# A mixture-of-experts stage whose low-row experts get plain transposes instead of a transposing matmul that adds

## The chip, the cores and the metric

One core of a Trainium2 chip runs the whole program. The metric is the device time of one execution in microseconds (us); a kernel's time is the median of its runs. TensorE (PE) does matmuls, with its weight loads shown as PEld; VectorE is DVE, ScalarE is ACT, GpSimd is POOL, SyncE is SP.

## The reference, cut to what matters

Two layer blocks run on 256 tokens of width 1024. The change lies in the last large step, a mixture of 8 experts in which each token goes to two of them:

```
def moe_swiglu(h, w_router, w1, w3, w2):
    t = h.reshape(B * S, D)
    ...
    for e in range(N_EXPERTS_2):
        out = out + gates[:, e:e + 1] * swiglu(t, w1[e], w3[e], w2[e])

def swiglu(h, w1, w3, w2):
    return (jax.nn.silu(h @ w1) * (h @ w3)) @ w2
```

w1 and w3 are 1024 x 3584 and w2 is 3584 x 1024 for each expert, all float32.

## The kernel before, in words

`moe` handles each expert's own tokens alone. `gather` collects them into at most 128 slots, as a high part (fp32r) and a low part (what fp32r lost); slot i*64+s stands at position 2s+i. Whether an expert has more than 64 rows is known only at run time, so matmuls stand twice, in the two arms of a branch that `arms` builds and TensorE's sequencer takes: "many" (over 64 rows) and "few". In the trace L1613 is the up matmul of many, L1610 that of few; L1641 is the transpose of many, L1639 its counterpart of few. By these lines experts 0, 1 and 4 have many rows here, and experts 2, 3, 5, 6 and 7 few.

An expert's 3584 hidden columns are done in two halves of 1792 (NS = 2); half number i is 2e+s for expert e, s = 0 or 1. A half is made of jobs of two weight tiles of 128 x 1792 (896 KB) each:

- 4 jobs of w1 and 4 of w3 ("up"). Each tile is loaded into `raw` (9 buffers), ScalarE rounds it into `whi` (L99), VectorE subtracts to get `wlo` (L100); 4 buffers of each. TensorE multiplies the gathered rows by both. In a few expert the 64 high rows and the 64 low rows lie side by side as one stationary operand of 128, so the product has the high rows' result on partitions 0 to 63 and the low rows' on 64 to 127, and the two have still to be added. `evict` copies w1's banks to `gs` and w3's to `us` (L1828).
- `turn`: `gs` and `us` are transposed in blocks of 128 x 128, 14 of each per half, in four pieces (8, 8, 8 and 4 blocks). For a many expert that is a transpose (L1641). For a few expert it is a matmul of the block with the constant `both` (L1639), whose even columns hold two ones, so that the two halves are added while the block is transposed; the result lies in even columns.
- `turned` follows each piece: ScalarE makes the silu of the gate's bank `pts[0]` into `sg` (L1822), and VectorE multiplies it by the other bank into `hd` (L1823). `hd` has one buffer, so the first write for half i waits until the down matmuls of half i-1 have read the last one.
- 4 jobs of w2 ("down", L1629), straight from `raw`, with `hd` as the stationary operand.

The order on TensorE is: up of half i with the four pieces of half i-1 among its w1 jobs, then down of half i-1, then up of half i+1. At s = 0 the pieces of the half before belong to another expert and have a branch of their own; at s = 1 they stand inside the branch of the up job. After the last half of an expert `finish` adds its result to the tokens (`dh`, `dl`, L1659, L1664). A scheduler decides the order within each engine; each engine then takes its instructions in that fixed order. Weight loads are issued by SP in the order of the jobs, each as soon as its buffer of `raw` is free.

In what follows a **stretch** runs from the first down matmul of one half to the first of the next: it has 8 down tiles and then 16 up tiles. A first-half stretch is one whose up tiles are of s = 0, a second-half stretch one of s = 1.

Of the kernel before, what the change touches and what calls it, by code (L numbers as in the profile page):

```python
# [8 lines left out]
F32 = mybir.dt.float32  # L9
# [3 lines left out]
AF = mybir.ActivationFunctionType  # L13
ALU = mybir.AluOpType
AX = mybir.AxisListType
PSUM = bass.MemoryType.PSUM
ADD, SUB, MUL = ALU.add, ALU.subtract, ALU.mult
MAX, MIN, EQ = ALU.max, ALU.min, ALU.is_equal

P = 128  # L20
# [1109 lines left out]
class Block2:  # L1130
# [378 lines left out]
    def moe(self, cap=P):  # L1509
# [4 lines left out]
        K, nc, tc, a, x = self.K, self.K.nc, self.K.tc, self.a, self.x  # L1514
        E, NS, HALF = 8, 2, P // 2
        MS, R = 1792, 7
        BANKS = ((0, 512), (512, 512), (1024, 512), (1536, 256))
        iota = iota_row(K, self.pool, P)

        both = self.T([P, P])  # L1520
        nc.gpsimd.memset(both[:, 1::2], 0.0)
        nc.vector.tensor_tensor(both[:, 0::2], K.ident[:, :HALF], K.ident[:, HALF:], op=ADD)
        up_of = lambda n, e, s, k: a[n][0, e, k * P:(k + 1) * P, s * MS:(s + 1) * MS]

        def down_of(e, s, j):
# [68 lines left out]
        def arms(e, f):  # L1594

            with tc.If(many[e] > HALF) as c:
                f(False)
            with c.Else():
                f(True)
# [15 lines left out]
        def up(few, e, g, to, k, w):  # L1615

            for b, (o, n) in enumerate(BANKS):
                piece(few, g[:, k], w, slice(o, o + n), to[b][:, :n], k == 0, k == KC - 1, b < 2)

        def down(few, s, hd, acc, j, w):  # L1620


            c0 = c = j % 4 * MS
            while c < c0 + MS:
                c1 = min((c // 512 + 1) * 512, c0 + MS)
                r, h = divmod(c // 512, 2)
                o = slice((r + h) % 2 * HALF, (r + h) % 2 * HALF + HALF) if few else slice(0, P)
                n = 2 if few else 1
                mm(acc[h][o, c % 512:c % 512 + c1 - c], hd[:, j // 4 * R + r, ::n], w[0][:, c - c0:c1 - c0],  # L1629
                   start=s == 0 and j < 4 and r < n and c % 512 == 0,  # L1630
                   stop=s == NS - 1 and j > 3 and r >= R - n and c1 % 512 == 0)
                c = c1

        def turn(few, rows, pt, c0):

            for c in range(c0, min(c0 + 4, 2 * R)):
                z = rows[:, c // R * (MS // 2) + c % R:(c // R + 1) * (MS // 2):R]
                if few:
                    mm(pt[:, (c - c0) * P:(c - c0 + 1) * P], z, both, start=True, stop=True)  # L1639
                else:  # L1640
                    nc.tensor.transpose(pt[:, (c - c0) * P:(c - c0 + 1) * P], z, K.ident)  # L1641

        def transposed(e, h):

# [159 lines left out]
        for t in range(NT):  # L1804
            with K.behind(K.last):
                top2_weights(K, self.tmp, *tops[t][:2], iota, comb[:, t, :])
                nc.gpsimd.tensor_scalar(x[:, t, :], x[:, t, :], ALPHA, None, op0=MUL)
        most, mosti = self.T([P, 1]), self.T([P, 1], I32)
        nc.vector.tensor_reduce(most, cnt, axis=AX.X, op=MAX)
        nc.vector.tensor_copy(mosti, most)  # L1810
# [5 lines left out]
        def turned(i, c, pts):  # L1816

            n = min(4, 2 * R - c) * P
            if c == 0:
                hT[i] = self.W([P, 2 * R, P], "hd", F32, 1)  # L1820
            sg = self.W([P, 512], "sg", bufs=1)
            nc.scalar.activation(sg[:, :n], pts[0][:, :n], AF.Silu)  # L1822
            nc.vector.tensor_tensor(hT[i].rearrange("p c s -> p (c s)")[:, c * P:c * P + n], sg[:, :n], pts[1][:, :n], op=MUL)  # L1823
# [7 lines left out]
        for n, (name, e, s, ks) in enumerate(jobs):  # L1831
# [4 lines left out]
            if name == "down":  # L1836
                if s == 0 and q == 0:
                    accs[e] = [K.ps() for _ in range(2)]
                if i == E * NS - 1 and q == 0:
                    for c in range(0, 2 * R, 4):  # L1840
                        pts = [K.ps() for _ in range(2)]
                        arms(e, lambda few: [turn(few, rows, pt, c) for rows, pt in zip(ups[i], pts)])
                        turned(i, c, pts)
                arms(e, lambda few: [down(few, s, hT[i], accs[e], *t) for t in tiles])
                if s == NS - 1 and q == 4:
                    hotT = transposed(e, gs[e][1])
                if s == NS - 1 and q == 6:
                    if e == E - 1:
                        finish_last(e, accs.pop(e), hotT)
                    else:  # L1850
                        ends = finish(e, accs.pop(e), hotT)
                        next(ends)
                continue
# [6 lines left out]
            before = first and i > 0  # L1860
            if before:
                pts = [K.ps() for _ in range(2)]
                turns = lambda few: [turn(few, rows, pt, 2 * q) for rows, pt in zip(ups[i - 1], pts)]
                if s == 0:

                    arms(e - 1, turns)

            def f(few):
                if before and s:
                    turns(few)  # L1870
                for t in tiles:
                    up(few, e, g, banks, *t)
            arms(e, f)
            if before:
                turned(i - 1, 2 * q, pts)
            if q == 6:
# [81 lines left out]
```

## Time and profile before

| | |
|---|---|
| median of 3 runs | 2000.67 us (1997.23 to 2002.16) |
| the profiled execution | 1999.19 us, of which 1997.6 us are the span from first to last instruction |
| PE busy | 1843.4 us (92%) |
| PEld, DVE, ACT, POOL busy | 1450.1, 1133.8, 929.9, 169.8 us |
| HBM read | 543 MB, 272 GB/s over the span |

The expert stage runs from about 942 us to 1958 us of the span. A busy PE is not one at its peak: a row of busy time also holds matmuls that wait for weight loads. Times in the rows below are us from the span's start.

### The profile page before, as it was taken

What the parts mean: (1) busy time and instruction counts of PE and PEld (TensorE: products, weight loads), DVE (VectorE), ACT (ScalarE), POOL (GpSimd) and SP (SyncE); (2) the same over time, 40 slices, a digit from 0 to 9 for tenths busy, and PEclk for the clock granted to TensorE, in tenths of its full rate; (3) what the DMA queues carried; (4) which work ended last, traced back from release to release, by engine and by line L of the source; (5) the groups of instructions that cost most, each with busy time, mean ns of one, the idle gap of its engine ahead of it and who ended that gap; (6) DMA issues with size and microseconds to landing.
All of it is one profiled execution on the core that took longest, in us unless ns stands there. A gap on an engine that the chain in (4) does not pass through costs nothing. (4 is left out here: it accounts for less than half of the span.)

```text
span 1997.6 us, 27678 instructions
## 1 busy us (share of the span) xinstructions
PE 1843.4 (92%) x11023; PEld 1450.1 (73%) x11023; DVE 1133.8 (57%) x1395; ACT 929.9 (47%) x1222; POOL 169.8 (9%) x251
## 2 busy tenths in 40 slices
PE   7988698877999999987999999999999999999997
PEld 6878464323779998776877677877878678787875
DVE  4765542111986555887756436656557455675635
ACT  6444341101474443555746445545555445565533
POOL 2051210000400000324100000000000000000002
PEclk9989789889999999998999999999999999999999
DMA  7000579999655554415888989899989898999982
GB/s 221 29 1 1 193 292 407 421 421 397 243 179 175 190 190 148 169 43 219 323 299 318 327 273 376 319 362 395 360 326 400 306 361 308 387 376 359 405 318 106
DMA packets 131002, 546.58 MB, mean 274 GB/s; under 512 B 13568, under 2 KB 46475, under 8 KB 118540
## 3 DMA queue, kind: packets, MB, share of 16 engines
q1 hardware_dynamic: 126604, 539.21, 71.6%
q10 hardware_dynamic: 3952, 3.84, 0.6%
q8 instruction: 129, 2.11, 0.4%
q0 software_dynamic: 272, 1.05, 0.2%
q14 instruction: 45, 0.37, 0.1%
HBM read 543.01 MB, written 1.05 MB: 272 GB/s over the span
## 5 line engine op out<-in xcount | busy, mean ns | idle before, releaser
L100 DVE TENSOR_TENSOR wlo<-raw,whi 128x1792 fp32r<-128x1792 f32 (+2 forms) x412 | 681.0, 1694 | 291.5 <-ACT whi L99 290.2
L99 ACT ACTIVATE whi<-raw 128x1792 fp32r<-128x1792 f32 (+3 forms) x436 | 582.1, 1382 | 175.6 <-DMA raw<-in_exp_w_dram 59.2
L1610 PE MATMUL ps<-wlo,xg 128*128 128x256 f32 (+1 forms) x960 | 266.5, 308 | 17.0 <-DVE wlo L100 16.7
L1629 PE MATMUL ps<-raw,hd 128*64 128x512 f32 (+3 forms) x1024 | 275.4, 541 | 0.9 <-DVE hd L1823 0.9
L1610 PE MATMUL ps<-whi,xg 128*128 128x256 f32 (+1 forms) x960 | 266.7, 308 | 0.0
L1613 PE MATMUL ps<-whi,xg 128*128 128x512 f32 (+1 forms) x768 | 225.3, 373 | 0.0
L1629 PEld LDWEIGHTS ps<-raw,hd 128*64 128x64 f32 (+1 forms) x1024 | 129.5, 158 | 127.5 <-issue 111.8
L1610 PEld LDWEIGHTS ps<-wlo,xg 128*128 128x128 f32 x960 | 187.8, 196 | 33.5 <-DVE wlo L100 27.2
L1610 PEld LDWEIGHTS ps<-whi,xg 128*128 128x128 f32 x960 | 188.8, 197 | 9.6 <-issue 2.9
L114 PE MATMUL ps<-xTl,whi 128*128 128x256 f32 x576 | 161.4, 282 | 1.4 <-DVE xTl L100 1.4
L1613 PEld LDWEIGHTS ps<-whi,xg 128*128 128x128 f32 x768 | 141.6, 190 | 27.5 <-issue 1.5
L115 PE MATMUL ps<-xTh,wlo 128*128 128x256 f32 x544 | 153.4, 283 | 3.3 <-DVE wlo L100 3.2
L113 PE MATMUL ps<-xTh,whi 128*128 128x256 f32 x544 | 151.4, 281 | 0.4 <-ACT xTh L99 0.4
L1613 PE MATMUL ps<-wlo,xg 128*128 128x512 f32 (+1 forms) x384 | 141.7, 369 | 0.7 <-DVE wlo L100 0.7
L100 POOL TENSOR_TENSOR wlo<-raw,whi 128x448 fp32r<-128x448 f32 (+3 forms) x24 | 39.4, 1666 | 1105.7 <-ACT whi L99 1105.6
L1823 DVE TENSOR_TENSOR hd<-sg,ps 128x512 f32<-128x512 f32 x64 | 39.5, 617 | 127.2 <-PE ps L1629 88.7
L114 PEld LDWEIGHTS ps<-xTl,whi 128*128 128x128 f32 x576 | 108.7, 189 | 3.5 <-DVE xTl L100 2.7
L1822 ACT ACTIVATE sg<-ps 128x512 f32<-128x512 f32 x64 | 34.5, 539 | 162.0 <-PE ps L1639 91.6
L115 PEld LDWEIGHTS ps<-xTh,wlo 128*128 128x128 f32 x544 | 104.0, 191 | 5.7 <-DVE wlo L100 5.6
L113 PEld LDWEIGHTS ps<-xTh,whi 128*128 128x128 f32 x544 | 102.3, 189 | 1.7 <-ACT xTh L99 0.9
L1105 PE MATMUL ps<-dn,hT 128*32 128x512 f32 x256 | 70.3, 664 | 19.2 <-DMA dn<-in_w_down_dram 19.2
L1613 PEld LDWEIGHTS ps<-wlo,xg 128*128 128x128 f32 x384 | 73.0, 190 | 15.0 <-DVE wlo L100 1.2
(525 smaller groups left out, 2722.9 us busy)
## 6 DMA issues: line engine op xcount, KB each, us to landing
raw<-in_exp_w_dram SPq DMA_DIRECT2D x384, 896.0 KB
raw<-in_dense_w_dram SPq DMA_DIRECT2D x33, 1024.0 KB
gu<-in_w_up_dram SPq DMA_DIRECT2D x32, 1024.0 KB
dn<-in_w_down_dram SPq DMA_DIRECT2D x32, 1024.0 KB
gu<-in_w_gate_dram SPq DMA_DIRECT2D x29, 1024.0 KB
raw<-in_w_in_dram SPq DMA_DIRECT2D x19, 1024.0 KB
raw<-in_w_out_dram SPq DMA_DIRECT2D x8, 1024.0 KB
raw<-in_ple_gate_w_dram SPq DMA_DIRECT2D x8, 1024.0 KB
```

The costliest lines, as they stand in the source:

```text
L99: self.last = [nc.scalar.activation(hi[o], src[o], AF.Copy).ins, (engine or nc.vector).tensor_tensor(lo[o], src[o], hi[o], op=SUB).ins]
L100: (engine or nc.vector).tensor_tensor(lo[o], src[o], hi[o], op=SUB).ins]
L113: mm(out, a[0], b[0], start=first, stop=False)
L114: mm(out, a[0], b[1], start=False, stop=False)
L115: return mm(out, a[1], b[0], start=False, stop=last).ins
L1105: nc.tensor.matmul(ps[32 * e:32 * e + 32, :], hT[:, k, 32 * e:32 * e + 32], wd[e][:, k, hs], start=(k == 0), stop=(k == 1))
L1610: mm(to[:, o:o + m], few_rows, w[q][:, i.start + o:i.start + o + m], start=first and o == 0 and q == 0, stop=last and o + m == n and q == 1)
L1613: mm(to, rows[:, a_], w[b_][:, i], start=first and q == 0, stop=last and q == 2)
L1629: mm(acc[h][o, c % 512:c % 512 + c1 - c], hd[:, j // 4 * R + r, ::n], w[0][:, c - c0:c1 - c0], start=s == 0 and j < 4 and r < n and c % 51 ...
L1822: nc.scalar.activation(sg[:, :n], pts[0][:, :n], AF.Silu)
L1823: nc.vector.tensor_tensor(hT[i].rearrange("p c s -> p (c s)")[:, c * P:c * P + n], sg[:, :n], pts[1][:, :n], op=MUL)
```

## The change

For a few expert the block is now transposed as for a many expert, with the identity. Behind each piece ScalarE copies the second half of each block's columns (partition 64 and up of the product, now columns 64 to 127) out of PSUM into `odd`, times `fewer`, a per-expert factor that is 1 for few and 0 for many; VectorE adds it to the first half in place, in PSUM. Both happen for every expert. Then silu and product follow as before. The down matmul of a few expert takes the first 64 columns of `hd` instead of the even ones. Since `turn` no longer depends on the expert, it needs no branch: the pieces stand outside of `arms`. The constant `both` goes.

```
-                mm(acc[h][o, c % 512:c % 512 + c1 - c], hd[:, j // 4 * R + r, ::n], w[0][:, c - c0:c1 - c0],
+                mm(acc[h][o, c % 512:c % 512 + c1 - c], hd[:, j // 4 * R + r, :P // n], w[0][:, c - c0:c1 - c0],
...
-        def turn(few, rows, pt, c0):
+        def turn(rows, pt, c0):
...
-                if few:
-                    mm(pt[:, (c - c0) * P:(c - c0 + 1) * P], z, both, start=True, stop=True)
-                else:
-                    nc.tensor.transpose(pt[:, (c - c0) * P:(c - c0 + 1) * P], z, K.ident)
+                nc.tensor.transpose(pt[:, (c - c0) * P:(c - c0 + 1) * P], z, K.ident)
...
+        fewer = self.T([P, E])
+        nc.vector.tensor_scalar(fewer, cnt, HALF + 0.5, None, op0=ALU.is_lt)
...
         def turned(i, c, pts):
...
+            for b, pt in enumerate(pts):
+                z = pt[:, :n].rearrange("p (c i s) -> p c i s", i=2, s=HALF)
+                odd = self.W([P, 4, HALF], f"odd{b}", F32, 1)[:, :n // P]
+                nc.scalar.activation(odd, z[:, :, 1], AF.Copy, scale=fewer[:, i // NS:i // NS + 1])
+                nc.vector.tensor_tensor(z[:, :, 0], z[:, :, 0], odd, op=ADD)
...
-                turns = lambda few: [turn(few, rows, pt, 2 * q) for rows, pt in zip(ups[i - 1], pts)]
-                if s == 0:
-
-                    arms(e - 1, turns)
-
-            def f(few):
-                if before and s:
-                    turns(few)
-                for t in tiles:
-                    up(few, e, g, banks, *t)
-            arms(e, f)
+                for rows, pt in zip(ups[i - 1], pts):
+                    turn(rows, pt, 2 * q)
+            arms(e, lambda few: [up(few, e, g, banks, *t) for t in tiles])
```

The built order shows two places. The first is TensorE's in expert 3's first half, between the first and the second down job of expert 2, where the first piece of half 5 stands. `ps` are the two PSUM banks of the piece, `t_8038` is `both`, `t_63` the identity. Before:

```order
L1596 COMPARE_AND_BRANCH
L1641 MATMUL ps_12377<-t_63,gs_11961 128x128 x4
L1641 MATMUL ps_12378<-t_63,us_12214 128x128 x4
L1596 UNCONDITIONAL_BRANCH
L1639 MATMUL ps_12377<-t_8038,gs_11961 128x128 x4
L1639 MATMUL ps_12378<-t_8038,us_12214 128x128 x4
L1596 UNCONDITIONAL_BRANCH
```

Now:

```order
L1592 UNCONDITIONAL_BRANCH
L1634 MATMUL ps_12348<-t_63,gs_11932 128x128 x4
L1634 MATMUL ps_12349<-t_63,us_12185 128x128 x4
L1592 COMPARE_AND_BRANCH
L1625 MATMUL ps_12243<-raw_12238,hd_11680 128x512
```

The piece is at the same place, without its branch and without the second arm.

The second place is VectorE's in expert 3's second half, from the start of the down jobs of half 5 on. Before, with `dl` the first step of expert 2's `finish`:

```order
L100 TENSOR_TENSOR wlo_13017<-raw_13014,whi_13016 128x1792
L100 TENSOR_TENSOR wlo_13023<-raw_13020,whi_13022 128x1792
L100 TENSOR_TENSOR dl_13044<-ps_12271,dh_13043 128x512
L1596 UNCONDITIONAL_BRANCH
L100 TENSOR_TENSOR wlo_13050<-raw_13047,whi_13049 128x1792
L100 TENSOR_TENSOR wlo_13056<-raw_13053,whi_13055 128x1792
L1823 TENSOR_TENSOR hd_13130<-sg_13131,ps_13064 128x512
```

Now:

```order
L1818 TENSOR_TENSOR ps_13027<-ps_13027,odd_2005_13088 128x4x64
L1592 UNCONDITIONAL_BRANCH x3
L100 TENSOR_TENSOR wlo_12980<-raw_12977,whi_12979 128x1792
L1823 TENSOR_TENSOR hd_13091<-sg_13092,ps_13027 128x512
L100 TENSOR_TENSOR wlo_12986<-raw_12983,whi_12985 128x1792
L100 TENSOR_TENSOR dl_13007<-ps_12242,dh_13006 128x512
L1592 UNCONDITIONAL_BRANCH
L100 TENSOR_TENSOR wlo_13013<-raw_13010,whi_13012 128x1792
L100 TENSOR_TENSOR wlo_13019<-raw_13016,whi_13018 128x1792
L1818 TENSOR_TENSOR ps_13107<-ps_13107,odd_2016_13166 128x4x64
```

The write of `hd` (L1823), which waits for the last down job, has moved ahead of the second `wlo`, and the additions (L1818) stand between the subtractions. In first-half stretches `hd` already stood behind the first `wlo` before.

## Rows read from the trace of the kernel before

**Rows 1.** Groups by line and form: busy us, mean ns | idle before and releasers.

```profile
L1639 PE MATMUL ps<-t,gs 128*128 128x128 f32 x280 | 71.4, 396 | 2.7 <-PEq L1699 2.7
L1641 PE MATMUL ps<-t,gs 128*128 128x128 f32 x84 | 14.3, 287 | 0.0
```

**Rows 2.** Timeline of PE, one piece of few, then one of many: start, us.

```profile
1261.58 1.89 PE L1639 MATMUL ps<-t,gs 128*128 128x128 f32 x8
1263.31 2.02 PE L1639 MATMUL ps<-t,us 128*128 128x128 f32 x8
1265.08 0.38 PE L1610 MATMUL ps<-whi,xg 128*128 128x256 f32 x1
...
990.50 0.65 PE L1641 MATMUL ps<-t,gs 128*128 128x128 f32 x4
990.99 0.74 PE L1641 MATMUL ps<-t,us 128*128 128x128 f32 x4
991.49 0.48 PE L1613 MATMUL ps<-whi,xg 128*128 128x512 f32 x1
```

**Rows 3.** Stretches: length, busy of PE, PEld, DVE, ACT, POOL, PEclk, DMA share, GB/s.

```profile
1237.53:1306.45 68.92, 68.92 (x354) 55.55 (x352) 39.16 (x30) 34.24 (x36) 0.00 (x0) 1.00 0.92 333
1306.45:1365.92 59.47, 56.14 (x315) 45.27 (x314) 34.93 (x25) 31.50 (x30) 0.00 (x0) 1.00 0.93 359
1365.92:1423.27 57.35, 57.35 (x354) 49.32 (x353) 39.16 (x30) 34.17 (x36) 0.00 (x0) 1.00 1.00 397
1423.27:1490.34 67.07, 66.36 (x316) 51.84 (x315) 34.84 (x25) 31.97 (x29) 0.00 (x0) 1.00 0.88 337
1550.94:1612.26 61.32, 57.42 (x288) 42.19 (x287) 34.84 (x25) 31.50 (x30) 0.00 (x0) 1.00 0.90 331
1740.66:1800.83 60.17, 57.43 (x353) 49.33 (x352) 39.27 (x30) 34.37 (x36) 0.00 (x0) 0.97 0.98 379
1859.90:1914.83 54.93, 54.92 (x321) 46.09 (x321) 37.74 (x26) 32.73 (x32) 0.00 (x0) 1.00 1.01 404
1914.83:1958.10 43.27, 40.72 (x188) 24.47 (x187) 3.42 (x8) 3.60 (x9) 0.00 (x0) 1.00 0.64 233
```

**Rows 4.** The same columns for parts of stretches: down, up, up, up.

```profile
1306.45:1323.53 17.08, 17.08 (x81) 9.53 (x80) 2.02 (x1) 8.06 (x8) 0.00 (x0) 1.00 0.81 290
1323.53:1365.92 42.39, 39.06 (x235) 35.74 (x234) 32.91 (x24) 23.44 (x22) 0.00 (x0) 1.00 0.97 387
...
1378.16:1423.27 45.11, 45.11 (x291) 43.51 (x289) 35.34 (x29) 29.99 (x31) 0.00 (x0) 1.00 1.01 400
...
1575.56:1612.26 36.70, 32.80 (x216) 29.21 (x215) 32.81 (x24) 23.36 (x22) 0.00 (x0) 1.00 1.00 395
```

**Rows 5.** VectorE's and ScalarE's groups by form, 945 to 1960 us.

```profile
L100 DVE TENSOR_TENSOR wlo<-raw,whi 128x1792 fp32r<-128x1792 f32 x252 | 499.4, 2021 | 214.2 <-ACT whi L99 212.9 <-ACTq L1699 0.9
...
L1823 DVE TENSOR_TENSOR hd<-sg,ps 128x256 f32<-128x256 f32 x16 | 6.7, 418 | 17.1 <-PE ps L1639 15.2 <-ACT sg L1822 1.8
...
L1822 ACT ACTIVATE sg<-ps 128x256 f32<-128x256 f32 x16 | 6.0, 375 | 27.3 <-PE ps L1639 20.1 <-PE ps L1641 7.2
```

**Rows 6.** Waits, 945 to 1960 us: total us, times, longest.

```profile
DVE hd L1823 <- PE ps L1629: 88.7, 8, 26.9
```

**Rows 7.** Timeline of DVE in a first-half stretch, then a second-half one.

```profile
1314.41 2.02 DVE L100 TENSOR_TENSOR wlo<-raw,whi 128x1792 fp32r<-128x1792 f32 x1 [9.72 <-ACT whi L99]
1323.66 0.69 DVE L1823 TENSOR_TENSOR hd<-sg,ps 128x512 f32<-128x512 f32 x1 [7.22 <-PE ps L1629]
...
1376.36 2.03 DVE L100 TENSOR_TENSOR wlo<-raw,whi 128x1792 fp32r<-128x1792 f32 x1 [0.17 <-ACT whi L99]
```

**Rows 8.** Timeline of PE at the end of the stage.

```profile
1933.52 6.29 PE L1629 MATMUL ps<-raw,hd 128*64 128x512 f32 x32
...
1944.27 1.19 PE L1639 MATMUL ps<-t,gs 128*128 128x128 f32 x4
```

**Rows 9.** The page's weight loads, and a full-rate 10 us (columns as in rows 3).

```profile
raw<-in_exp_w_dram SPq DMA_DIRECT2D x384, 896.0 KB
...
1700.00:1710.00 10.00, 9.26 (x56) 8.84 (x55) 8.19 (x6) 3.77 (x3) 0.00 (x0) 1.00 1.01 422
```

More of the change, by code (lines that the diff above doesn't have):

```diff
@@ L1518, in moe @@
         iota = iota_row(K, self.pool, P)
-        both = self.T([P, P])
-        nc.gpsimd.memset(both[:, 1::2], 0.0)
-        nc.vector.tensor_tensor(both[:, 0::2], K.ident[:, :HALF], K.ident[:, HALF:], op=ADD)
         up_of = lambda n, e, s, k: a[n][0, e, k * P:(k + 1) * P, s * MS:(s + 1) * MS]
@@ L1841, in moe @@
                         pts = [K.ps() for _ in range(2)]
-                        arms(e, lambda few: [turn(few, rows, pt, c) for rows, pt in zip(ups[i], pts)])
+                        for rows, pt in zip(ups[i], pts):
+                            turn(rows, pt, c)
                         turned(i, c, pts)
```

## The prediction

> **What bounds the kernel now.** I read the groups by line first, then cut the expert stage into stretches (windows whose edges are the first down matmuls), then asked in each stretch which engine leaves no time free.
>
> The groups show what the change removes [rows 1]: 280 passes of L1639 on `gs` and as many on `us`, which are two passes for each of 280 blocks, that is 10 halves of 28 blocks: five few experts. The timeline shows what a piece costs [rows 2]: eight blocks of few take from 1261.58 to 1265.08, 3.50 us; eight plain transposes of many take from 990.50 to 991.49, 0.99 us. So a full piece becomes 2.5 us shorter on TensorE and the short fourth piece half of that, 1.25 us; a half's four pieces 8.75 us, and all ten halves 87.5 us. That would be the gain if TensorE bounded every stretch.
>
> It doesn't. A stretch loads 24 tiles of 896 KB, 22.0 MB, and the stream's best rate is 422 GB/s [rows 9], so no stretch can average less than 52.2 us. The stretches of few rows take 55 to 60 us [rows 3]. And the split of the weights is a third limit. The clearest row is the up part from 1575.56 to 1612.26 [rows 4]. Its up tiles are of few rows, but the pieces among them are of many rows, so plain transposes; it is what the up part of a few stretch becomes when TensorE's pieces get short. It takes 36.70 us, PE is busy for 32.80, and VectorE for 32.81: VectorE's 16 subtractions of 1.98 us (499.4 / 252 [rows 5]) fill it but for 3.9 us, in which the split passes between ScalarE, VectorE and TensorE. VectorE can't do them in advance. In first-half stretches it makes one `wlo` in the down part and then stands at `hd`, which waits for the last down matmul [rows 7]: the wait of 7.22 us there, and 88.7 us in 8 waits in all [rows 6]. In second-half stretches it has two done by then: the row at 1376.36 is the second, and 1378.16 is where the up part starts [rows 4, 7].
>
> **What the change does, part by part.**
>
> *Transposes:* priced above by a many piece on the same kind of data in the same place of the code, so I take 2.5 us a piece as it stands. The Trainium skill is less hopeful (TensorE: Matmul & The Clock Gate, "Part 4: PE-mode transpose"): it puts a 128 x 128 transpose at some 275 ns in a kernel's context, mostly latency. By that, an estimate, a piece of eight takes 2.2 us and saves 1.3 us instead of 2.5. The row's spacing is 0.12 us a block; only its duration column, 287 ns, looks like the page's figure, and the transposes overlap.
>
> *Additions:* each of the 64 pieces gets two ScalarE copies and two VectorE additions, of 256 columns or, in the fourth piece, 128. The trace has no such addition. The nearest rows are `hd` of 256 columns, PSUM and SBUF in, 418 ns, and `sg` of 256 columns out of PSUM, 375 ns [rows 5]. From below a `wlo`'s time per column bounds it, 2.02 / 1792 x 256 = 0.29 us, since an added instruction can't cost nothing on a full engine; from above the 0.69 us that the timeline shows for an `hd` of twice the columns [rows 7]. I take 0.42 us, nearest in size and operands, and 0.28 for the short ones: a half costs VectorE 3.1 us, of which three pieces, 2.2 us, fall in the up part, and 0.4 us for the next half's early `gs` addition: 2.6. ScalarE gets about 2.8 us a half; it is busy 23 of 42 us there [rows 4], so its own time is covered, unless it stands waiting (below).
>
> *The moved `hd`:* in second-half stretches `hd` now stands behind the first `wlo`. Behind it wait all other `wlo`, and TensorE's up tiles wait for those. The wait itself costs nothing, as TensorE is busy with down matmuls, but one `wlo` less is ready when the up part starts: 2.0 us more for VectorE there.
>
> *Branches:* 32 fewer, inside the pieces' measured times. *Down matmuls* read 64 adjacent columns instead of every second one: same passes, nothing counted. A gain there is not excluded, but all eight down tiles take 12.24 us, from 1365.92 to 1378.16 [rows 3, 4], which is less than the stream needs for eight tiles, 17.4 us.
>
> Now the stretches, with the up part as VectorE's work plus the unfilled 3.9 us:
>
> - First-half stretches of few rows with few pieces (1306.45, and two like it to within 0.4 us): down 17.08 - 2.5 = 14.6; up 32.91 + 2.6 + 3.9 = 39.4 instead of 42.39 [rows 4]; together 54.0, above the stream's 52.2. Gain 5.5 us each, 5.1 in the shortest: 16.1 us.
> - The stretch at 1423.27 (few pieces, then up tiles of many rows): TensorE is busy for 66.36 of 67.07 us and stays the bound. Gain 8.75 us.
> - Second-half stretches of few rows (1237.53 and one like it, 1365.92, 1740.66, 1859.90): up 35.34 + 2.0 + 2.2 + 3.9 = 43.4 instead of 45.11, which is the row at 1378.16; the down part gets the first piece's 1.0 us and some 0.5 us for being split by it. Net 0.2 us, counted as nothing; in the last, whose VectorE work is 1.4 us less but whose length is already 54.93, I count 0.7 us lost.
> - Up parts of few rows behind many pieces (1575.56, in the stretch of 61.32 us, and one like it before): no shorter pieces, but 2.6 us of additions where VectorE is the bound: 5.2 us lost.
> - Stretches of many rows alone: TensorE-bound; additions are hidden, the later `wlo` costs some tenths. 1 us lost in all.
> - The end of the stage, 1914.83 to 1958.10: down, four few pieces, down, with VectorE busy for 3.42 us. The pieces save 8.75. The last down jobs of half 14 end at about 1939.8 and the fourth piece stands only behind the next job [rows 8]; the chain of `hd` writes behind keeps its length. I take 9 us.
>
> Sum: -16.1 - 8.75 + 0.7 + 5.2 + 1 - 9 = -27 us. The profiled execution took 1999.19 us, 1.5 below the median, so the sum gives **1972 us**. Of TensorE's 87.5 us less than a third reaches the end.
>
> **The rivals.**
>
> *1. VectorE isn't the limit* (chance 0.17). Then each stretch falls by 8.75 us until the stream stops it at 52.2: the three first-half ones by 7.3, 7.3 and 6.9, second-half ones by 8.75 twice, 5.1, 8.0 and 2.7, the one at 1423.27 and the end by 8.75 and 9: 72 us, or 1927. For it: in today's second-half up parts VectorE has 10 us free, and 3.9 us need not be needed everywhere. Against it: the 36.70 us row, which has short pieces and still takes that long.
>
> *2. Hand-offs, slower* (0.22). Each piece is now a chain ScalarE, VectorE, ScalarE, VectorE, and each link sits in a queue among splits of 1.7 and 2.0 us. If a `sg` waits behind a `wlo` for its addition, the `whi` behind it is late and VectorE idles. Place: the up parts of few rows, ten of them. If the unfilled 3.9 us double, that is 39 us: 2011. The point of decision is 2.7 us more in each; at half the price it would be 1992. For it: three of these links in every up part, and a split of 2 us ahead of each. Against it: VectorE is nearly full in any case, so the `sg` finds its addition done when VectorE is late anyway.
>
> *3. The clock* (0.04). In the row at 1740.66 the granted clock is 0.97 over 60 us: about 3.6 us at the lower level, 1.2 GHz, behind a wait for weights, where PE was idle for 2.7 us [rows 3]. More waiting of TensorE, up to 9 us in 54, could bring more such falls: each costs 1.8 us of matmuls, and with one for each of the 30 pieces in those ten up parts 54 us: 2026. Against it: in the 36.70 us row PE is idle as often and the clock stands at 1.00. The Trainium skill, too, speaks against the change here (TensorE: Matmul & The Clock Gate, "Part 4: PE-mode transpose"): transposes don't count as busy time for the clock gate in the way that matmuls do. The row with plain transposes and few-row matmuls, 1.00 at 1575.56 [rows 4], doesn't show it.
>
> **How the numbers follow.** My forecast has 0.57, with a range of its own from 1958 to 1984. The 3.9 us of slack and the price of an addition (0.29 to 0.69, some 2 us a stretch) are what it hangs on. Rival 1 gives the lower side, rival 2 the upper. The range 1938 to 1999 leaves out half of rival 1 and some 0.11 of rivals 2 and 3. A change under 0.3%, 6 us, can hardly be told from none in this kernel: three runs of before lie 5 us apart. Faster than that: 0.57 + 0.17 + a quarter of rival 2, 0.80; within it 0.07; slower 0.13.
>
> **What would show it.** A piece of few at 1.0 us on TensorE, and no L1639-like second pass. VectorE's wait of `hd` for the down matmuls up from 8 times to about 15. The up part at 1306.45's place at 39 to 40 us with VectorE free for about 4; the second-half stretches unchanged within 2 us; the stretch at 1423.27's place near 58. Wrong would be: second-half stretches at 53 us with VectorE free (rival 1), or VectorE free for 7 us and more in up parts while ScalarE waits for additions (rival 2).

## The result, and the profile after

The changed kernel takes 1971.01 us (median of 4 runs, 1969.67 to 1975.02), the kernel before 1998.95 us beside it (4 runs): a ratio of 0.9864, 95% interval 0.984 to 0.9888. The profiled execution took 1970.95 us with a span of 1969.3, against 1999.19 and 1997.6: 28.3 us less of span.

The groups by line and form of the changed kernel, to be read against [rows 1, 5]. TensorE first (L1634 is now the transpose of both kinds of expert), then ScalarE's copies and VectorE's additions:

```profile
L1634 PE MATMUL ps<-t,us 128*128 128x128 f32 x224 | 41.1, 299 | 20.2 <-DVE hd L1823 12.5 <-DVE t L1657 4.2 <-ACT us L1828 2.9
L1634 PE MATMUL ps<-t,gs 128*128 128x128 f32 x224 | 39.0, 290 | 2.7 <-PEq L1692 2.4 <-DVE t L1657 0.4
...
L1817 ACT ACTIVATE odd<-ps,t 128x256 f32<-128x256 f32 x96 | 45.1, 472 | 165.3 <-PE ps L1634 165.1
L1817 ACT ACTIVATE odd<-ps,t 128x128 f32<-128x128 f32 x32 | 10.7, 366 | 10.7 <-PE ps L1634 10.7
...
L1818 DVE TENSOR_TENSOR ps<-ps,odd 128x256 f32<-128x256 f32 x96 | 39.5, 426 | 128.2 <-ACT odd L1817 127.6
L1818 DVE TENSOR_TENSOR ps<-ps,odd 128x128 f32<-128x128 f32 x32 | 8.5, 291 | 3.3 <-ACT odd L1817 3.3
```

An addition costs 426 ns and a short one 291, where the prediction took 0.42 and 0.28 us; ScalarE's copy takes 472 instead of 375 ns. New is what stands behind the bars: TensorE's transposes wait 12.5 us for `hd`, since the next piece needs the PSUM bank that the last product still reads. The timeline of TensorE shows two pieces of a few expert, the second with such a wait, to be read against [rows 2]:

```profile
1332.66 0.66 PE L1634 MATMUL ps<-t,gs 128*128 128x128 f32 x4
1333.16 0.66 PE L1634 MATMUL ps<-t,us 128*128 128x128 f32 x4
1333.57 0.37 PE L1606 MATMUL ps<-whi,xg 128*128 128x256 f32 x1
...
1336.98 0.67 PE L1634 MATMUL ps<-t,gs 128*128 128x128 f32 x4
1338.83 0.73 PE L1634 MATMUL ps<-t,us 128*128 128x128 f32 x4 [1.18 <-DVE hd L1823]
```

Eight blocks take 0.91 us, from 1332.66 to 1333.57, instead of 3.50: some 0.11 us a block. The Trainium skill puts a 128 x 128 transpose at some 275 ns in a kernel's context (TensorE: Matmul & The Clock Gate, "Part 4: PE-mode transpose"). By that, an estimate, eight would take 2.2 us; the trace doesn't agree, and the measurement decides.

The stretches of the changed kernel, in the order and with the columns of [rows 3]:

```profile
1246.49:1313.84 67.35, 62.29 (x323) 46.20 (x321) 40.94 (x37) 35.73 (x42) 0.00 (x0) 1.00 0.93 327
1313.84:1366.74 52.90, 47.16 (x292) 36.34 (x291) 37.92 (x34) 35.61 (x40) 0.00 (x0) 1.00 1.01 405
1366.74:1423.37 56.63, 51.75 (x321) 39.92 (x321) 40.95 (x37) 35.75 (x42) 0.00 (x0) 1.00 1.02 413
1423.37:1480.47 57.10, 57.10 (x292) 42.79 (x291) 37.99 (x34) 35.42 (x39) 0.00 (x0) 1.00 0.99 390
...
1542.82:1606.50 63.68, 57.69 (x292) 42.69 (x291) 37.99 (x34) 35.36 (x40) 0.00 (x0) 1.00 0.91 332
...
1726.35:1784.50 58.15, 51.55 (x326) 41.44 (x325) 41.56 (x38) 36.60 (x44) 0.00 (x0) 0.97 1.00 400
...
1837.38:1891.02 53.64, 48.41 (x290) 36.37 (x289) 39.44 (x33) 34.54 (x38) 0.00 (x0) 1.00 1.02 416
1891.02:1928.37 37.35, 32.86 (x160) 15.25 (x159) 6.56 (x16) 6.95 (x17) 0.00 (x0) 0.95 0.66 262
```

Row by row against [rows 3] the changes are -1.6, -6.6, -0.7, -10.0, +2.4, -2.0, -1.3 and -5.9 us. Where TensorE was busy for 56 of 59 us it is now busy for 47 of 53, and the DMA share stands at 1.00: the first thing that one suspects now is the stream of weights. The down part and the up parts, to be read against [rows 4] (first-half down, first-half up, second-half up, few up behind many pieces):

```profile
1313.84:1328.19 14.35, 14.35 (x73) 6.72 (x72) 2.89 (x3) 7.85 (x10) 0.00 (x0) 1.00 0.98 372
1328.19:1366.74 38.55, 32.81 (x220) 29.62 (x219) 35.02 (x31) 27.75 (x31) 0.00 (x0) 1.00 1.01 417
1380.60:1423.37 42.77, 37.89 (x253) 33.69 (x253) 38.49 (x35) 31.11 (x36) 0.00 (x0) 1.00 1.02 413
1569.78:1606.50 36.72, 30.74 (x205) 27.89 (x206) 33.35 (x30) 26.39 (x30) 0.00 (x0) 1.00 0.99 379
```

The first-half up part takes 38.55 us with VectorE free for 3.5; the forecast was 39.4 and 3.9. VectorE's wait of `hd` [rows 6] and its timeline in that stretch [rows 7] became:

```profile
DVE hd L1823 <- PE ps L1625: 111.9, 14, 13.9
```

```profile
1318.72 0.93 DVE L1818 TENSOR_TENSOR ps<-ps,odd 128x256 f32<-128x256 f32 x2 [6.70 <-ACT odd L1817]
1321.78 2.03 DVE L100 TENSOR_TENSOR wlo<-raw,whi 128x1792 fp32r<-128x1792 f32 x1 [2.13 <-ACT whi L99]
1328.32 0.69 DVE L1823 TENSOR_TENSOR hd<-sg,ps 128x512 f32<-128x512 f32 x1 [4.51 <-PE ps L1625]
```

The wait stands in 14 places instead of 8, behind one finished `wlo`.

Two places lost what the forecast did not count. Near the start of the stage the transposes now stand ahead of the second part of the down matmuls, right behind the eviction whose result they read; TensorE waits, and the granted clock falls behind that wait (timeline of TensorE, then windows with the columns of [rows 3]):

```profile
1052.96 1.13 PE L1634 MATMUL ps<-t,us 128*128 128x128 f32 x4 [2.64 <-ACT us L1828]
```

```profile
1049.80:1052.90 3.10, 0.53 (x4) 0.32 (x2) 0.43 (x1) 2.04 (x5) 0.00 (x0) 1.00 0.98 314
1052.90:1056.30 3.40, 3.34 (x7) 1.93 (x8) 0.51 (x2) 2.94 (x6) 0.00 (x0) 0.50 0.29 122
```

For 3.4 us the clock is 0.50, the lower level, 1.2 GHz. And at the end of the stage the fourth piece is a chain of its own (against [rows 8]): transposes at 1912.44, copy, addition, `sg`, `hd`, and only then the next use of `sg`, on which the last down matmuls wait:

```profile
1908.85 3.65 PE L1625 MATMUL ps<-raw,hd 128*64 128x512 f32 x16 [0.80 <-DVE hd L1823]
1912.44 0.51 PE L1634 MATMUL ps<-t,us 128*128 128x128 f32 x2
1915.96 0.43 PE L1643 MATMUL ps<-t,sg 128*128 128x128 f32 x2 [3.01 <-DVE sg L1642]
```

Behind this wait, too, the clock falls:

```profile
1916.50:1919.90 3.40, 3.40 (x12) 1.26 (x12) 0.35 (x1) 0.00 (x0) 0.00 (x0) 0.50 0.02 7
```

### The profile page after: what moved, and what is told of

It reads as the page before. It is cut to its first block, busy times and chain, and to the rows that moved or that the text cites. A ratio compares the mean times of both kernels' runs of the same rounds, so it can differ in the third digit from the quotient of the medians.

```text
span 1969.3 us, 27368 instructions
## 1 busy us (share of the span) xinstructions
PE 1771.9 (90%) x10743; PEld 1358.7 (69%) x10743; DVE 1174.0 (60%) x1523; ACT 972.2 (49%) x1350; POOL 170.3 (9%) x250
## 5 line engine op out<-in xcount | busy, mean ns | idle before, releaser
L1606 PE MATMUL ps<-wlo,xg 128*128 128x256 f32 (+1 forms) x960 | 271.4, 312 | 31.4 <-DVE wlo L100 31.4
L1625 PE MATMUL ps<-raw,hd 128*64 128x512 f32 (+3 forms) x1024 | 281.8, 547 | 0.8 <-DVE hd L1823 0.8
L1606 PEld LDWEIGHTS ps<-wlo,xg 128*128 128x128 f32 x960 | 188.2, 196 | 54.3 <-DVE wlo L100 47.6
L1609 PEld LDWEIGHTS ps<-whi,xg 128*128 128x128 f32 x768 | 141.6, 190 | 28.3 <-issue 2.1
L1817 ACT ACTIVATE odd<-ps,t 128x256 f32<-128x256 f32 (+1 forms) x128 | 55.8, 445 | 176.1 <-PE ps L1634 175.8
L1818 DVE TENSOR_TENSOR ps<-ps,odd 128x256 f32<-128x256 f32 (+1 forms) x128 | 47.9, 393 | 131.5 <-ACT odd L1817 130.9
L1823 DVE TENSOR_TENSOR hd<-sg,ps 128x512 f32<-128x512 f32 x64 | 39.4, 616 | 114.1 <-PE ps L1625 111.9
L1105 PE MATMUL ps<-dn,hT 128*32 128x512 f32 x256 | 69.6, 650 | 20.2 <-DMA dn<-in_w_down_dram 20.1
```

Of the source, the lines that this page charges most:

```text
L1105: nc.tensor.matmul(ps[32 * e:32 * e + 32, :], hT[:, k, 32 * e:32 * e + 32], wd[e][:, k, hs], start=(k == 0), stop=(k == 1))
L1606: mm(to[:, o:o + m], few_rows, w[q][:, i.start + o:i.start + o + m], start=first and o == 0 and q == 0, stop=last and o + m == n and q == 1)
L1609: mm(to, rows[:, a_], w[b_][:, i], start=first and q == 0, stop=last and q == 2)
L1817: nc.scalar.activation(odd, z[:, :, 1], AF.Copy, scale=fewer[:, i // NS:i // NS + 1])
L1818: nc.vector.tensor_tensor(z[:, :, 0], z[:, :, 0], odd, op=ADD)
```

## The experiments

Three sessions, each with its own runs of the kernel before: 1998.42, 1997.81 and 1998.77 us, close enough for medians of different sessions to be set side by side. Theory V is the prediction's: VectorE's queue sets the few up parts, and the additions cost what they add to it. Theory S came from the DMA share of 1.00: the stream of weights bounds the few stretches now. The time ahead of the stage differs by up to 5.5 us between the profiled executions of the table (TensorE's 9.09 us of idle time ahead of it begins at 931.64 in the changed kernel and at 935.99 in the run without additions), so places are compared by stretch:

| stretch, start in before | before | changed | no_additions | transposes_alone | hd_two_buffers | half_loads |
|---|---|---|---|---|---|---|
| many, 1103.78 | 72.37 | 73.06 | 73.30 | 75.17 | 72.76 | 77.82 |
| few behind many pieces, 1176.15 | 61.38 | 63.55 | 61.34 | 62.03 | 62.32 | 64.00 |
| second half, 1237.53 | 68.92 | 67.35 | 67.17 | 65.76 | 66.14 | 67.31 |
| first half, 1306.45 | 59.47 | 52.90 | 50.67 | 50.66 | 51.89 | 52.33 |
| second half, 1365.92 | 57.35 | 56.63 | 56.80 | 55.87 | 56.82 | 57.19 |
| few pieces, many up, 1423.27 | 67.07 | 57.10 | 58.46 | 58.02 | 56.96 | 57.60 |
| many, 1490.34 | 60.60 | 62.35 | 62.59 | 63.42 | 62.19 | 67.68 |
| few behind many pieces, 1550.94 | 61.32 | 63.68 | 61.35 | 61.30 | 62.45 | 63.97 |
| second half, 1612.26 | 68.93 | 67.33 | 67.17 | 65.74 | 66.14 | 67.18 |
| first half, 1681.19 | 59.47 | 52.52 | 50.68 | 50.65 | 56.46 | 51.80 |
| second half, 1740.66 | 60.17 | 58.15 | 58.53 | 60.79 | 55.59 | 56.63 |
| first half, 1800.83 | 59.07 | 52.88 | 50.60 | 51.05 | 51.88 | 51.93 |
| second half, 1859.90 | 54.93 | 53.64 | 52.60 | 51.64 | 54.13 | 55.19 |

**no_additions.** The changed kernel without its copies and additions, so that the low rows of a few expert are left out of its sums:

```
-                nc.scalar.activation(odd, z[:, :, 1], AF.Copy, scale=fewer[:, i // NS:i // NS + 1])
-                nc.vector.tensor_tensor(z[:, :, 0], z[:, :, 0], odd, op=ADD)
```

> The changed kernel without its ScalarE copies and VectorE additions (so the low rows of a few expert are left out of its sums). Theory V, VectorE's work bounds the up parts of few rows: each of the ten loses its 2.6 us of additions, and the end of the stage its short links: 26 to 30 us less, about 1943 us. Theory S, the weight stream now bounds the few stretches (DMA share 0.99 to 1.02 in six of seven of them): only the two up parts of few behind many pieces, the stretches at 56.6 to 58.2 us and the end can give something: 5 to 12 us less, 1959 to 1966 us; the stretches at 52.5 to 52.9 us stay within 0.7 us.

Measured: 1956.55 us, ratio 0.9785 (0.9767 to 0.9803): 14.5 us less than the change, between the two theories. By place V is borne out: the three first-half stretches fall by 2.2, 1.8 and 2.3 us, the two few ones behind many pieces by 2.2 and 2.3; S held the first three fixed. Four of the five second-half ones don't move (0.2, -0.2, 0.2, -0.4, and 1.0 in the last): there the additions cost nothing that shows, and V, as I had stretched it to ten up parts, is wrong. That isn't proof that VectorE doesn't set these stretches when the additions are there, for something else comes late without them. The waits of ScalarE and VectorE in the stretch of 56.63 us of the changed kernel, then in the same one, 56.80 us, of no_additions:

```profile
ACT whi L99 <- DMA raw<-in_exp_w_dram: 3.3, 2, 2.8
DVE wlo L100 <- ACT whi L99: 6.0, 3, 4.1
...
ACT whi L99 <- DMA raw<-in_exp_w_dram: 10.1, 2, 9.9
DVE wlo L100 <- ACT whi L99: 16.9, 3, 14.2
```

Without additions ScalarE waits 9.9 us for one load to land, and VectorE 14.2 us for what ScalarE makes of it.

From the first down matmul of the last half to the end of the span it is 3.6 us, and ahead of the first down of the second half, (1109.88 - 931.64) - (1110.34 - 935.99) = 3.9 us: without additions the 2.64 us wait isn't there.

**fewer_loads** and **half_loads.** Two ways to cut the stream by a sixth: every second down tile uses the tile before it once more, or down tiles bring half of their columns, which are read twice. Both leave half of the down weights out of the result. The edit of the first:

```
-                taken[n] = [take(name, e, s, k) for k in ks]
+                taken[n] = [take(name, e, s, k) for k in ks[:1 if name == "down" else 2]]
+                if name == "down":
+                    taken[n].append((ks[1], taken[n][0][1]))
```

> The changed kernel with 20 weight loads in a half instead of 24: every second down tile multiplies the tile loaded before it once more (so half of the down weights are not used). TensorE, VectorE and ScalarE do the same instructions. Theory S, the stream bounds the few stretches: its floor falls from 52.2 to 43.5 us, and the seven few stretches shorten until TensorE (47.1 us busy in a first-half one) or VectorE bounds them, by 3 to 6 us each: 20 to 40 us less, 1931 to 1951 us. Theory V, VectorE's chain bounds them: stretches within 1 us of the changed kernel's, 1965 to 1971 us.

> The changed kernel with down tiles of half the size: each of the eight loads for a half's down matmuls brings 448 KB instead of 896, and the matmuls read its columns twice (so half of the down weights are left out). The instructions of all engines and their order stay, the stream falls from 24 to 20 tiles a half, a floor of 43.5 us. Theory V+S: first-half few stretches, which VectorE bounds, stay within 1 us (52.5 to 52.9); second-half few ones at 56.6 and 58.2 us, in which ScalarE waits for loads to land, lose 1 to 4 us each: 2 to 10 us less, 1961 to 1969. Theory S alone: all seven few stretches lose 3 to 6 us: 1931 to 1951. Theory V alone: no change, 1969 to 1972.

Measured: 1979.96 us, ratio 0.9907 (0.9891 to 0.9924), and 1980.86, ratio 0.9917 (0.9903 to 0.993): 9 and 10 us *more* than the change, which no theory had. The two stretches of half_loads at the changed kernel's 52.90 and 56.63 us (columns of [rows 3]):

```profile
1316.97:1369.30 52.33, 46.89 (x292) 35.75 (x291) 38.54 (x35) 37.14 (x40) 0.00 (x0) 1.00 0.90 345
1369.30:1426.49 57.19, 52.23 (x321) 40.27 (x320) 40.70 (x37) 33.56 (x38) 0.00 (x0) 0.97 0.89 329
```

The DMA share is down to 0.90, and the stretches are as long as they were, to 0.6 us: a share of 1.00 did not mean that the stream was the bound. For first-half stretches S falls; no_additions, with all the bytes, is even shorter there (50.67 us). The expected gain in second-half stretches didn't come either, but there the row says less: its clock of 0.97 is some 3.4 us at the lower level, worth up to 1.7 us, and the additions still stand in it. Additions and bytes were not taken out together. The loss is elsewhere, 5.3 us in the many stretch at 1490.34 and 4.8 in the one at 1103.78: the scheduler, given other loads, put the instructions in another order (VectorE's `hd` waits for down matmuls 3 times, 9.3 us in all, instead of 14 times). In each of these two TensorE now waits 2.2 us for `sg`, and the granted clock is 0.97 and 0.98 where it was 1.00. So these runs test the stream in the few stretches and say nothing on the sum.

**hd_two_buffers** and **raw_eight.** A second `hd` buffer, paid for by one of `raw`, and the control with that payment alone:

```
-                hT[i] = self.W([P, 2 * R, P], "hd", F32, 1)
+                hT[i] = self.W([P, 2 * R, P], "hd", F32, 2)
...
-RAW = 9
+RAW = 8
```

> The changed kernel with two hd buffers, paid for by one raw buffer less (8 instead of 9): hd no longer waits for the down matmuls (111.9 us in 14 waits in the changed kernel). Theory V: VectorE makes one to three wlo during the down part, which takes 2 to 4 us from each of ten up parts of few rows: 20 to 40 us less, 1931 to 1951. Theory S: the stream is as long, and with 8 buffers in place of 9 it runs less far ahead: between 5 us less and 10 us more, 1966 to 1981.

> The changed kernel with 8 raw buffers instead of 9 and one hd buffer: the control for the two hd buffers. If the stream's lead matters: 2 to 8 us more than the change, 1973 to 1979, and the second hd buffer is worth that on top of its 8.7. If it doesn't: within 2 us of the change, 1969 to 1973, and the 8.7 us are the second hd buffer's alone.

Measured: 1962.32 us, ratio 0.9818 (0.9801 to 0.9836), and 1969.93, ratio 0.9858 (0.9842 to 0.9873). The ninth `raw` buffer is worth nothing that shows, and the second `hd` buffer 8 us: this version leaves nothing out and is faster than both kernels. V had the sign, but its 20 to 40 us are two to five times the size. VectorE's timeline in the first-half stretch, whose up part starts at 1323.49:

```profile
1315.12 0.69 DVE L1823 TENSOR_TENSOR hd<-sg,ps 128x512 f32<-128x512 f32 x1 [0.17 <-ACT sg L1822]
1318.99 2.02 DVE L100 TENSOR_TENSOR wlo<-raw,whi 128x1792 fp32r<-128x1792 f32 x1 [3.18 <-ACT whi L99]
1321.45 2.03 DVE L100 TENSOR_TENSOR wlo<-raw,whi 128x1792 fp32r<-128x1792 f32 x1 [0.44 <-ACT whi L99]
1324.85 2.03 DVE L100 TENSOR_TENSOR wlo<-raw,whi 128x1792 fp32r<-128x1792 f32 x1 [1.36 <-ACT whi L99]
```

`hd` doesn't wait any more and two `wlo` are done instead of one, but the stretch gains only 1.0 us: now VectorE waits for ScalarE's `whi` (110.1 us in 106 waits over the stage, against 66.4 in 76). The first-half stretch at 1681.19 even became 3.9 us longer, with a wait of TensorE of 5.5 us for a `wlo` and a granted clock of 0.97.

**hd_later.** The `turned` of a half's first piece written one job later in the program.

> The changed kernel with the additions, sg and hd of a half's first piece written one job later (behind the next two splits) in program order. Theory V: VectorE makes two wlo more while the down matmuls run, so the up part of few starts with more ready: 1 to 3 us less in each of ten, 1941 to 1961. Theory S: within 4 us of the changed kernel, as the stream sets the few stretches. A rival for both: the second piece's transposes wait for the banks of the first, and TensorE stands 1 to 2 us more in each stretch: up to 30 us more, 2001.

Measured: 1970.80 us, ratio 0.9861 (0.9842 to 0.988), the changed kernel's time. Nothing follows: VectorE's rows came out of the scheduler in the same order, with other buffer numbers.

**branches_kept, transposes_alone, additions_alone.** With no_additions they make a table of what was changed by parts. The first puts the plain transposes back into the branches of before:

```
-                for rows, pt in zip(ups[i - 1], pts):
-                    turn(rows, pt, 2 * q)
-            arms(e, lambda few: [up(few, e, g, banks, *t) for t in tiles])
+                turns = lambda few: [turn(rows, pt, 2 * q) for rows, pt in zip(ups[i - 1], pts)]
+                if s == 0:
+                    arms(e - 1, turns)
+            def f(few):
+                if before and s:
+                    turns(few)
+                for t in tiles:
+                    up(few, e, g, banks, *t)
+            arms(e, f)
```

The second is the same without copies and additions; the third is the kernel before with copies and additions behind its own transposing matmuls, `fewer` being 0.

> The changed kernel with its plain transposes put back inside the branches of before (the same code in both arms), so that they stand where before had them among the up and down tiles; additions as in the change. Theory O, the new order costs: the first half loses its 2.64 us wait for the evicted us and the lower clock behind it (about 6 us), the stretch at 1480.47 its 1.7 us, hd waits for the down matmuls about 8 times again instead of 14, and the few up parts of second halves start with one wlo more (2 us in four of them): 10 to 16 us less than the change, 1955 to 1961. Rival N, the order costs nothing outside the first half: 4 to 6 us less, 1965 to 1967; the 32 branches more than in the change cost under 1 us.

> The kernel before with plain transposes in its branches and no additions (the low rows of a few expert are left out of its sums): the transposes' share of the change alone. Additive theory: the changed kernel loses 14.5 us of additions (the run without them), and the branches cost 7.8 us more where they are kept: 1956.6 + 7.8 = 1964 us, 1960 to 1968. Rival: the 7.8 us are a fight between additions and the old order, as the additions cost 27 us in the kernel before; without additions the old order costs nothing: 1952 to 1958.

> The kernel before with the additions of the change put behind its own transposes with a factor of 0 throughout (the result is the same). Theory V: TensorE's long pieces hide most of it; the two few up parts behind many pieces take 2.2 us more each, first-half few up parts, where VectorE was free 9.5 of 42 us, up to 1 us each, and the end 1 to 3: 4 to 10 us more than before, 2002 to 2008. Rival H, the chain through ScalarE and VectorE costs in every piece wherever it stands: 0.5 to 1 us in 64 pieces, 30 to 60 us more, 2028 to 2058.

| median us | no additions | with additions |
|---|---|---|
| transposing matmuls, branches | 1998 (before) | 2024.93, ratio 1.0142 (1.0127 to 1.0158) |
| plain transposes, branches | 1956.82, ratio 0.9792 (0.9778 to 0.9806) | 1978.81, ratio 0.9905 (0.989 to 0.992) |
| plain transposes, no branches | 1956.55 | 1971.01 (the change) |

The transposes alone give 42 us, and dropping the branches adds nothing to that. The additions cost 27, 22 and 14 us, from top to bottom: theory O, that the new order costs, has the wrong sign in the sum, and the additive theory is wrong. The branches matter only with additions. By place O is right in four of the five second-half few stretches: in branches_kept `hd` doesn't wait there for the down matmuls, and they take 65.5, 53.9, 65.1 and 51.6 us, 1.8, 2.7, 2.2 and 2.0 less than in the change (the one at 1740.66 takes 3.4 more). Elsewhere it loses more than that. Two waits of TensorE in branches_kept:

```profile
PE ps L1606 <- ACT sg L1822: 15.5, 9, 2.4
...
PE ps L1609 <- ACT sg L1822: 4.8, 2, 2.4
```

Up tiles wait 20.3 us in 11 places for `sg`, at the far end of a piece's chain; such a row is not there in the changed kernel, nor in transposes_alone. Why an up tile in a branch has to wait for it was not tried. Nor is it all: the transposes and `finish` wait 17.9 us for `t` (L1657), against 4.6 in the change, and the clock falls. From the first down matmul to the last, transposes_alone and then branches_kept (columns of [rows 3]):

```profile
1030.41:1913.50 883.09, 829.26 (x4446) 621.33 (x4445) 523.74 (x390) 466.74 (x441) 0.00 (x0) 0.99 0.94 362
1032.97:1934.52 901.55, 834.63 (x4424) 627.19 (x4423) 559.54 (x508) 504.69 (x559) 0.00 (x0) 0.97 0.93 354
```

Of the 18.5 us between them 13.1 are idle time of TensorE and 5.4 are busy time for the same matmuls. The clock record of branches_kept has 12 falls to 0.50 in that time, 47.8 us together, against 3 falls and 13.7 us in transposes_alone and 3 and 10.2 us in the changed kernel. Five of the 12 begin within 2 us of the end of a wait for `sg`, as at 1595.75, where a wait of 2.39 us ends, and 1595.8, where the clock falls. What the waits would cost at the higher level was not separated.

**add_twice.** A second addition, of zeros, behind each.

```
+                nc.vector.tensor_tensor(z[:, :, 0], z[:, :, 0], zero[:, :n // P], op=ADD)
```

> The changed kernel with a second VectorE addition (of zeros, same size) behind each of its additions; ScalarE's copies stay as they are. Theory V, VectorE's own time is the price: 0.86 us a piece, 2.2 us more in each of the up parts of first-half few stretches and the two behind many pieces, 1 us at the end, less elsewhere: 12 to 16 us more than the change, 1983 to 1987. Theory H, the hand-off to ScalarE and back is the price and VectorE's time is covered by its waits: 0 to 5 us more, 1971 to 1976.

Measured: 1994.68 us, ratio 0.9982 (0.9973 to 0.9991), 23.7 us more than the change and more than either theory. The first-half stretches at 1306.45 and 1681.19 grow by 1.8 and 1.2 us, those behind many pieces by 1.5 and 1.4: VectorE's time, nearly as V has it. More of it is in stretches of many rows (2.5 and 3.8 us, and some 3 ahead of them), where V had nothing, and there it is a hand-off (waits of TensorE):

```profile
PE ps L1634 <- ACT sg L1825: 25.7, 14, 2.5
```

The next piece's transposes need the banks of the last, and these come free one addition later. The 14 waits are spread over the stage; in a stretch of many rows, where TensorE has hardly any other idle time, one of 2.52 us is paid in full. Behind four of them the clock falls. The remaining 8 us or so lie in the stretch at 1423.27 (1.8), the last second-half one (2.0), the pair at 1740.66 and 1800.83 (3.1 together, as the edge between them moved) and smaller ones, and were not traced.

**gpsimd_split.** One up tile in eight is split by GpSimd:

```
-                taken[n] = [take(name, e, s, k) for k in ks]
+                taken[n] = [take(name, e, s, k, **({"engine": nc.gpsimd} if k == 5 and name != "down" else {})) for k in ks]
```

> The changed kernel with one of eight up tiles of each weight (32 of 256, two in each half) split by GpSimd instead of VectorE; GpSimd is idle in these stretches. A 128x448 part took GpSimd some 1.7 us, so a tile takes 6 to 7 us there, and 4 us of VectorE's 32 in an up part are gone. Theory V: the first-half few stretches (52.5 to 52.9) and the two few up parts behind many pieces each lose 2 to 4 us, second-half ones nothing because the loads come late there (ScalarE's whi waits for the DMA): 10 to 20 us less, 1951 to 1961. Rival P: GpSimd's 6 to 7 us come late for the tile or slow VectorE beside it: 1968 or more, with TensorE waiting for the GpSimd wlo.

Measured: 2025.42 us, ratio 1.014 (1.0124 to 1.0155): 54 us more than the change. The groups:

```profile
L100 DVE TENSOR_TENSOR wlo<-raw,whi 128x1792 fp32r<-128x1792 f32 x220 | 486.0, 2230 | 109.9 <-ACT whi L99 109.0 <-ACTq L1692 0.9
...
L100 POOL TENSOR_TENSOR wlo<-raw,whi 128x1792 fp32r<-128x1792 f32 x30 | 127.5, 4250 | 828.9 <-ACT whi L99 677.6 <-PE ps L1634 151.3
```

GpSimd takes 4.25 us a tile; my 6 to 7 us came from a mean of 1.7 us over parts of several sizes, of which the 128x448 ones take 1.23 us. VectorE's own tiles rise from 2020 to 2230 ns in the mean, 46 us over 220 of them. Both reasons of rival P are there: TensorE also waits 43.7 us in 20 places for GpSimd's tiles (34.6 in up tiles of few rows, 9.1 in those of many). The granted clock, from the first down matmul to the last, is 0.97, against 0.99 in the change; the three were not separated. The Trainium skill has the rule (SBUF — State Buffer, "Who interferes with whom"): a VectorE instruction with two SBUF inputs contends with a GpSimd instruction that reads SBUF. The trace agrees as far as it goes: the subtractions, with two such inputs, got longer, and the additions, with one input in PSUM, stay at 427 ns.

**split_five.** Five buffers of `whi` and `wlo` for two of `raw` (`RAW = 7`).

> The changed kernel with five buffers for each half of a split weight instead of four, paid for by two raw buffers (7 instead of 9). Theory V with the hand-offs: ScalarE and VectorE may be one tile further ahead when the up part starts, which is 1 to 2 us in each of ten few up parts: 8 to 15 us less than the change, 1956 to 1963. Theory S: with 7 loads in flight or waiting the stream falls short: 5 to 20 us more, 1976 to 1991.

Measured: 1976.22 us, ratio 0.9877 (0.9861 to 0.9892), 5 us more. Not explained: the order moved as well.

## Why the prediction was right, and where its terms were not

The mechanism held in part: of TensorE's 87.5 us a third reaches the end, and in first-half few stretches and behind many pieces the additions cost what VectorE's queue says. But 36.5 of the 59 us that don't arrive are missing in the five second-half few stretches (43.75 us taken off TensorE, 7.2 arrived), and there VectorE's part is not shown. That the sum came within 2 us of the measured 28.2 us of span is luck: the terms below miss by some 13 us to one side and 12 to the other.

- *Transposes and additions:* 0.91 us a piece for a forecast of 1.0, 426 and 291 ns for 0.42 and 0.28 us.
- *First-half few stretches:* forecast -16.1, measured -6.6, -7.0 and -6.2, together -19.7. The form "VectorE's work plus 3.9 us" is right with the additions (38.55 us for 39.4) and without them: 32.91 + 3.9 = 36.8, measured 36.3 (1326.51 to 1362.82 in no_additions). The second doesn't tell VectorE from TensorE, whose shorter pieces alone give 42.39 - 6.25 = 36.1. What was wrong is the stream's 52.2 us as a floor for a single stretch: without additions these take 50.7 us, at 398 GB/s, which is 20.2 MB and not 22.0, so two of the 24 tiles' worth had come before.
- *The stretch at 1423.27:* -8.75, measured -10.0; TensorE is its bound as said.
- *Few up parts behind many pieces:* +5.2, measured +2.2 and +2.4, and no_additions gives it back: the additions and nothing else.
- *Second-half few stretches:* 0 and a loss of 0.7 in the last, measured -1.6, -0.7, -1.6, -2.0 and -1.3, together -7.2. This is the largest miss. The 2.0 us for the moved `hd` are borne out by branches_kept in four of the five. The 2.2 us of additions are not: no_additions shortens one of the five, and branches_kept less transposes_alone is -0.2, -2.0, -0.7, 0.7 and 0.0 us. What bounds these stretches is open: without additions the loads come late, with fewer bytes the additions are left, and `hd`'s wait is only part of it (-1.2 us at 1237.53 with two buffers, but +0.2 at 1365.92). At 1365.92 itself the parts came out nearly as forecast, up part 42.77 us for 43.4, down part 13.86 for 13.7.
- *Many rows alone:* 1 us forecast; measured +6.1 in the first half with a start 0.4 later, +0.7 and +1.7. I took additions and order as hidden where TensorE is busy, and missed that a transpose moved ahead of the down matmuls stands right behind its own input. no_additions gives 3.9 of it back; some 2 us and the +1.7 are not settled, for the stretch at 1490.34 is as long without additions (62.59) and with branches (63.42).
- *The end:* -9, measured -5.9, and the rest behind the stage is 1.5 longer. The chain behind the last pieces did not keep its length: two links were added to each, and 3.01 us of waiting with 3.4 us of the lower clock behind them stand at its end. Without additions 3.6 us of it come back. The 1.5 us are in most variants (not in half_loads, and only a third of them in additions_alone) and were not traced.

Rival 1 was half right, which the forecast alone would not have shown: take the additions out, and the first-half stretches lose 8.8, 8.8 and 8.5 us, all that TensorE's pieces had given. Rival 2's hand-offs exist, 1 to 3 us at a time, and are dear where a branch or a second addition lengthens the chain. The clock (rival 3) fell for 3.4 us behind the two waits shown above and, as it had before the change, in the stretch of 58.15 us (0.97), not in thirty pieces; the first-half few stretches show 1.00. That third fall isn't behind a wait for weights, as the prediction had it: TensorE stands at a transpose and waits for its own sequencer (PEq), 2.74 us until 1755.71 before the change, and after it:

```profile
1741.01 0.73 PE L1634 MATMUL ps<-t,gs 128*128 128x128 f32 x4 [2.35 <-PEq L1692]
```

In the variants rival 3 is more than that: where a branch or a second addition makes TensorE wait some 2.5 us again and again, the clock falls behind many of these waits (branches_kept, add_twice).

## What to carry to other kernels

Work taken off a saturated engine is worth its full time only as far as the next engine's queue, so a swap has two prices: here 42 us for the transposes and 14 back for the additions, and the second depends on what stands around it (14, 22 or 27 us for the same instructions). A DMA share of 1.00 says that transfers are in flight; whether they are the bound is another question: cut the bytes and look at one stretch. Where taking out either of two suspects changes nothing, take out both before clearing them. When a scheduler sets the order, look first at whether an edit moved more than was meant, and look for a single-buffered tile that an added link now holds longer: one more `hd` buffer gave 8 us.

## What was not expected of the hardware

- A GpSimd subtraction of two SBUF operands beside VectorE's made VectorE's 128x1792 subtraction 2230 ns in the mean instead of 2020; one at 1356.07 took 2.65 us beside a GpSimd tile at 1352.79 of 4.04 us.
- TensorE's waits of 2.35, 2.64 and 3.01 us in the changed kernel were each followed by 3.4 us at a granted clock of 0.50. With TensorE busy for nearly all of it, each cost, by estimate, up to 1.7 us more than its own length.
- 128x128 float32 transposes follow one another every 0.11 us or so (eight in 0.91 us), though each has a duration of 290 to 299 ns.
